# S5 output loads and conv-state stores moved from SyncE's queue to GpSimd's, with three buffers for the conv states

## Chip, cores and metric

The kernel runs on one core of one Trainium2 chip. The metric is the device time of one execution in microseconds (us); lower is better. A profile has times of the engines TensorE (PE, with PEld for its weight loads), VectorE (DVE), ScalarE (ACT), GpSimd (POOL) and SyncE (SP). SP computes nothing here; its queue issues transfers (DMAs), and so do parts of POOL's.

## What is computed

One layer of a hybrid decoder for 320 tokens (256 of a prompt, 8 samples of 8 tokens) of width 2048, in float32:

```python
def hybrid_layer(x, conv_buf, h_re, h_im, ...):
    xn = rmsnorm(x, norm_mix)
    proj = xn @ w_in
    c_val = proj[..., :D_CONV]
    c_gate = proj[..., D_CONV:2 * D_CONV]
    s_in = proj[..., 2 * D_CONV:]
    yc, new_buf = conformer_conv(c_val, c_gate, conv_buf, ...)
    ys, nh_re, nh_im = s5_mixer(s_in, h_re, h_im, ...)
    mix = jnp.concatenate([rmsnorm(yc, gnorm_conv), rmsnorm(ys, gnorm_ssm)], axis=-1) @ w_out
    h = x + mix.astype(x.dtype)
    hn = rmsnorm(h, norm_ffn)
    ff = (jax.nn.silu(hn @ w_ffn_gate) * (hn @ w_ffn_up)) @ w_ffn_down
    h = h + ff.astype(x.dtype)
    return h, new_buf, nh_re, nh_im
```

`conformer_conv` multiplies c_val by sigmoid(c_gate), runs a causal convolution of width 31 over each of 1024 channels, a LayerNorm over the channels and silu; `new_buf` holds the last 30 input rows of the convolution and is an output (the conv state). `s5_mixer` runs a complex diagonal state-space scan in 64 groups of 16 channels, and then `y = gelu(y)` and `y * sigmoid(y @ w_glu)`. A final norm follows the layer.

## The kernel before

Every matrix product is done with float32 split into a high and a low part. The weights come in "subs" of 1024 columns over 128 partitions: a transfer on SP's queue brings the raw weights (L124, four buffers), ACT copies the high part (`hi`, L141), DVE subtracts it for the low part (`lo`, L142), and 24 matmuls multiply high by high, high by low and low by high (L166 to L168) into `mm`. The subs follow each other for the input projection (`xhl` times w_in), the GLU (`gehl` times w_glu, 4 subs for each of two groups of columns), the output projection of the S5 half (`mid`) and of the convolution half (`half`, `half2`), and the FFN.

Beside the projection run the two mixers. The convolution works in eight chunks `c` of 128 channels (`conv_chunk`, L380 to L420). For each chunk ACT and PE build the window `u` (in a `ubuf`), and PE transposes the last 30 rows of each sequence (L392), which ACT copies to the tile `uo` (L394); two stores bring `uo` to the outputs (L395, L396). Chunks 3 and 5 then run their 31 taps on DVE (L438, into `convy`). The other six go to PE: four transfers copy shifted pieces of the window to `ub` (L402, one buffer), and 64 matmuls over the prompt (L410) and 64 over the samples (L414) add up the taps in `cx`, which ACT moves to `convy` (L419). `stn` (L377) is the load of the old conv state.

The S5 half works in eight blocks of 128 channels. Its end stores the block's result to DRAM (`yd`, L842). `gelu` (L864 to L883) then loads it back in another layout: at blocks 0 and 4 eight transfers of 16x32x40 each fill the tile `yl` with four blocks (L870), and for each block ACT and DVE compute the gelu (`gsq` L875 and L876, `gz` L878 and L879, `ge` L881) and split it into `gehl`, the high part on ACT (L882) and the low part on DVE (L883). The GLU's matmuls need `gehl`.

After the last chunk the convolution's LayerNorm runs (`ln_mean` to `ln_end`, on DVE and ACT). Each norm ends with small matmuls that sum over the channels (L324), a chain of small DVE steps for the reciprocal root (`rv` to `rg`, L303 to L328), small matmuls that spread it (L316) and a copy (L318, `Rc` for the convolution's last norm). The output projection's conv half needs `Rc` for its results (L1021).

Every engine and every queue does its instructions in the order in which a scheduler put them when the kernel was built. `when(slot)` gives an instruction its priority (a table of slots for the parts of the mixers, `P_CONV` and the like), and the scheduler places an instruction by that and by the time at which it expects the inputs. So a transfer that is moved to another queue also moves other instructions in the order of every engine. POOL's queue carries, beside small set-up work, transfers of the S5 half (`ud` L725, `us` L727, `KTd` L808, `tst` L812) and, late, four loads of `h` (L1001).

Of the kernel before, what the change touches and what calls it, by code (L numbers as in the profile page):

```python
# [8 lines left out]
F32 = mybir.dt.float32  # L9
# [52 lines left out]
def kernel(ctx: ExitStack, tc: tile.TileContext,  # L62
# [7 lines left out]
    V, A, G, T, SP = nc.vector, nc.scalar, nc.gpsimd, nc.tensor, nc.sync  # L70
# [3 lines left out]
    @contextmanager  # L74
    def when(slot):

        old = tc.cur_priority
        tc.cur_priority = int(BASE + slot * SLOT)
        yield
        tc.cur_priority = old  # L80
# [13 lines left out]
    def sx_tile(shape):  # L94
        return pss.tile(shape, F32, tag="sx", name="sx")

    def cx_tile(shape):
        return pss.tile(shape, F32, tag="cx", name="cx", bufs=1)
# [105 lines left out]
    def pv(i):  # L204
        return PV[:, i:i + 1]
# [4 lines left out]
    convp = cpool.enter_context(tc.tile_pool(name="convp", bufs=1))  # L210
# [169 lines left out]
    def conv_chunk(c):  # L380
        u = us_.pop(c)
        traced.add(("conv", c))
        stn = stn_.pop(c)
        win_ = u[:, 350:654].rearrange("p (b t) -> p b t", t=38)
        A.activation(win_[:, :, 30:38], u[:, 286:350].rearrange("p (b t) -> p b t", t=8), AF.Copy)
        pc = sx_tile([128, 368])
        ps = pc[:, 0:240].rearrange("p (h r) -> p h r", h=2)
        for h in range(2):
            T.transpose(ps[:, h, :], stn[:, h, :], ident[:120, :120])
        A.activation(win_[:, :, 0:30], ps.rearrange("p h (b t) -> p (h b) t", t=30), AF.Copy)  # L390
        ps = pc[:94, 240:368]
        T.transpose(ps, u[:, 256:350], ident)  # L392
        uo = convp.tile([94, 128], F32, name="uo", bufs=1)
        A.activation(uo, ps, AF.Copy)  # L394
        SP.dma_start(ncv_p[0, 0, :, c * 128:(c + 1) * 128], uo[0:30])  # L395
        SP.dma_start(ncv_s[0, :, 22:30, c * 128:(c + 1) * 128], uo[30:94])  # L396
        if c in V_CONV:
            return conv_taps_on_v(c, u, win_)

        ub = convp.tile([128, 4, UW - 24], F32, name="ub", tag="wide")  # L400
        for b in range(4):
            SP.dma_start(ub[:, b, :],  # L402
                         bass.AP(tensor=u.tensor, offset=u[32 * b:32 * b + 32].offset,
                                 ap=[[u.ap[0][0], 32], [8, 4], [1, UW - 24]]))
        cw = cw_.pop(c)
        with when(P_CONV[c]):
            acc = cx_tile([128, NTOK])
            for k in range(8):
                for b in (3, 2, 1, 0):
                    T.matmul(acc[32 * b:32 * b + 32, 0:256], cw[:, b, k, :], ub[:, b, k:k + 256],  # L410
                             start=(k == 0), stop=False, skip_group_check=True)
            for k in range(8):
                for b in range(4):
                    T.matmul(acc[32 * b:32 * b + 32, 256:320].rearrange("p (b t) -> p b t", t=8),  # L414
                             cw[:, b, k, :],
                             bass.AP(tensor=ub.tensor, offset=ub[:, b, 350 + k:351 + k].offset,
                                     ap=[list(ub.ap[0]), [38, 8], [1, 8]]),
                             start=False, stop=(k == 7), skip_group_check=True)
            A.activation(convy[:, c, :], acc, AF.Identity, bias=pv(CB + c))  # L419
        add_ysum(c)  # L420

    def add_ysum(c):
        if c == 0:
            V.tensor_copy(ysum, convy[:, 0, :])
        else:
            V.tensor_tensor(ysum, ysum, convy[:, c, :], op=OP.add)

    def conv_taps_on_v(c, u, win_):

        pairs = [(convy[:, c, 0:256], lambda k: u[:, k:k + 256]),  # L430
                 (convy[:, c, 256:320].rearrange("p (b t) -> p b t", t=8),
                  lambda k: win_[:, :, k:k + 8])]
        for dst, src in pairs:
            A.activation(dst, src(0), AF.Identity, bias=pv(CB + c), scale=convw[:, c, 0:1])  # L434
        for k in range(1, 31):
            with when(P_CONV[c] + V_CONV[c] * k):
                for dst, src in pairs:
                    V.scalar_tensor_tensor(dst, src(k), convw[:, c, k:k + 1], dst,  # L438
                                           op0=OP.mult, op1=OP.add)
        with when(P_CONV[c] + V_CONV[c] * 31):  # L440
            add_ysum(c)
# [422 lines left out]
    def gelu(b):  # L864
        gp = late["gp"]
        ge, gehl = late["ge"], late["gehl"]
        if b % 4 == 0:
            yls = late["yl"] = gp.tile([128, 32, 40], F32, name="yl", bufs=2)
            for g in range(8):
                SP.dma_start(yls[16 * g:16 * g + 16],  # L870
                             bass.AP(tensor=yd.tensor, offset=yd.offset + b * 128 * NTOK + 40 * g,
                                     ap=[[NTOK, 16], [16 * NTOK, 32], [1, 40]]))
        yl = late["yl"][:, 8 * (b % 4):8 * (b % 4) + 8]
        sq = gp.tile([128, 8, 40], F32, name="gsq", bufs=3)
        A.activation(sq, yl, AF.Square)  # L875
        A.activation(sq, sq, AF.Copy, bias=C0, scale=C0 * 0.044715)  # L876
        z = gp.tile([128, 8, 40], F32, name="gz", bufs=3)
        V.tensor_tensor(z, sq, yl, op=OP.mult)  # L878
        A.activation(z, z, AF.Sigmoid)  # L879
        gv = ge[:, b, :].rearrange("p (j t) -> p t j", t=8)[:, ::-1, :]  # L880
        V.tensor_tensor(gv, z, yl, op=OP.mult)  # L881
        A.activation(gehl[:, 0, b, :], ge[:, b, :], AF.Copy)  # L882
        V.tensor_tensor(gehl[:, 1, b, :], ge[:, b, :], gehl[:, 0, b, :].bitcast(F32), op=OP.subtract)  # L883
# [428 lines left out]
    def post(b):  # L1312
# [3 lines left out]

    job(n_proj, open_mid)
    parts_ = dict(v=pool_v, pre=pre, e=s5_e, w=pool_w, scan=s5_scan, post=post, gelu=gelu,
                  stn=conv_states, cw=conv_weights, conv=conv_chunk, sample=lambda b: s5_sample_states(),
                  incoming=lambda b: s5_incoming(),  # L1320
                  states=lambda b: s5_states(), open_g=lambda b: open_g(),
# [75 lines left out]
```

## Time and profile before

| | us |
|---|---|
| median of 3 runs | 1400.57 |
| lowest, highest run | 1400.56, 1404.74 |
| the profiled execution | 1397.38 |
| its span, first to last instruction | 1395.6 |
| mean granted TensorE clock in it | 0.993 |

The profile describes one execution. Its span lacks 1.78 us that lie around the first and the last instruction. An engine's busy time is the sum of its instructions; times in a timeline are counted from the span's start. In a timeline one row can stand for several instructions of the same form in a row (x8), and the brackets at its end give the idle time of the engine just before it and what ended that idle time. For a queue a row is the issue of a transfer, not its landing.

### The profile page before, as it was taken

What the parts mean: (1) busy time and instruction counts of PE and PEld (TensorE: products, weight loads), DVE (VectorE), ACT (ScalarE), POOL (GpSimd) and SP (SyncE); (2) the same over time, 40 slices, a digit from 0 to 9 for tenths busy, and PEclk for the clock granted to TensorE, in tenths of its full rate; (3) what the DMA queues carried; (4) which work ended last, traced back from release to release, by engine and by line L of the source; (5) the groups of instructions that cost most, each with busy time, mean ns of one, the idle gap of its engine ahead of it and who ended that gap; (6) DMA issues with size and microseconds to landing.
All of it is one profiled execution on the core that took longest, in us unless ns stands there. A gap on an engine that the chain in (4) does not pass through costs nothing.

```text
span 1395.6 us, 24894 instructions
## 1 busy us (share of the span) xinstructions
PE 1370.2 (98%) x10246; PEld 1341.8 (96%) x10246; DVE 827.2 (59%) x1523; ACT 557.2 (40%) x813; POOL 30.3 (2%) x61
## 2 busy tenths in 40 slices
PE   8999999899999999999999999999999999999996
PEld 7999988889999999999999999999999999999996
DVE  7988899887888543543454444343544444444465
ACT  7445444464545333333333333333332233333332
POOL 0121010000000000000000000000000000000000
PEclk9999999999999999999999999999999999999998
DMA  9974475767434444444444444444444444454442
GB/s 256 234 153 148 161 210 159 162 173 236 137 127 160 151 151 151 148 148 148 148 149 151 151 151 151 147 154 150 145 146 153 151 150 151 151 181 151 152 136 76
DMA packets 146586, 220.12 MB, mean 158 GB/s; under 512 B 32377, under 2 KB 57529, under 8 KB 146328
## 3 DMA queue, kind: packets, MB, share of 16 engines
q1 hardware_dynamic: 143336, 208.50, 48.6%
q0 software_dynamic: 3136, 10.03, 2.8%
q8 instruction: 80, 1.31, 0.4%
q14 instruction: 34, 0.28, 0.1%
HBM read 201.04 MB, written 10.41 MB: 152 GB/s over the span
## 4 chain that ended last, share of the span: by engine, by line
PE 79%; DMA 3%; DVE 2%; SPq 1%; ACT 1%; issue 0%; DVEq 0%; ACTq 0%
PE mm L166 25%; PE mm L167 25%; PE mm L168 25%; DMA ub<-ubuf 1%; PE cx L410 1%; DVE lo L142 1%; PE sx L831 0%; DMA yl<-yd 0%; SPq L402 0%; PE sx L836 0%; DVE ge L881 0%; DMA tst<-KTd 0%; DVE convy L438 0%; SPq L870 0%; PE cx L414 0%
## 5 line engine op out<-in xcount | busy, mean ns | idle before, releaser
L142 DVE TENSOR_TENSOR lo<-raw,hi 128x1024 fp32r<-128x1024 f32 x352 | 429.8, 1223 | 428.1 <-ACT hi L141 427.3
L141 ACT ACTIVATE hi<-raw 128x1024 fp32r<-128x1024 f32 x352 | 372.6, 1060 | 638.5 <-PE mm L167 579.3
L166 PE MATMUL mm<-hn,hi 128*128 128x320 f32 x1408 | 434.9, 309 | 0.0
L167 PE MATMUL mm<-hn,hi 128*128 128x320 f32 x1408 | 434.8, 309 | 0.0
L168 PE MATMUL mm<-hn,lo 128*128 128x320 f32 x1408 | 431.2, 309 | 0.0
L166 PEld LDWEIGHTS mm<-hn,hi 128*128 128x128 f32 x1408 | 264.3, 188 | 0.1
L167 PEld LDWEIGHTS mm<-hn,hi 128*128 128x128 f32 x1408 | 264.3, 188 | 0.0
L168 PEld LDWEIGHTS mm<-hn,lo 128*128 128x128 f32 x1408 | 263.3, 188 | 0.0
L166 PE MATMUL mm<-aout,hi 128*128 128x320 f32 (+1 forms) x704 | 216.7, 308 | 0.0
L167 PE MATMUL mm<-aout,hi 128*128 128x320 f32 (+1 forms) x704 | 216.3, 308 | 0.0
L168 PE MATMUL mm<-aout,lo 128*128 128x320 f32 (+1 forms) x704 | 213.9, 307 | 0.0
L167 PEld LDWEIGHTS mm<-aout,hi 128*128 128x128 f32 x704 | 132.2, 188 | 0.0
L166 PEld LDWEIGHTS mm<-aout,hi 128*128 128x128 f32 x704 | 132.2, 188 | 0.0
L168 PEld LDWEIGHTS mm<-aout,lo 128*128 128x128 f32 x704 | 131.5, 188 | 0.0
L167 PE MATMUL mm<-xhl,hi 128*128 128x320 f32 x384 | 119.7, 314 | 0.3 <-DVE xhl L274 0.3
L168 PE MATMUL mm<-xhl,lo 128*128 128x320 f32 x384 | 119.5, 314 | 0.0
L166 PE MATMUL mm<-xhl,hi 128*128 128x320 f32 x384 | 115.8, 315 | 0.5 <-DVE vt L964 0.3
L167 PEld LDWEIGHTS mm<-xhl,hi 128*128 128x128 f32 x384 | 72.1, 188 | 1.6 <-issue 0.6
L166 PEld LDWEIGHTS mm<-xhl,hi 128*128 128x128 f32 x384 | 70.6, 188 | 2.3 <-issue 0.8
L168 PEld LDWEIGHTS mm<-xhl,lo 128*128 128x128 f32 x384 | 72.0, 188 | 0.8 <-issue 0.2
L1100 DVE TENSOR_TENSOR h<-mm,h 128x320 f32<-128x320 f32 (+1 forms) x64 | 29.8, 483 | 39.9 <-PE mm L168 39.9
L438 DVE SCALAR_TENSOR_TENSOR convy<-ubuf,convw,convy 128x256 f32<-128x256 f32 (+1 forms) x120 | 41.5, 380 | 2.3 <-ACT convy L434 1.7
(333 smaller groups left out, 1361.9 us busy)
## 6 DMA issues: line engine op xcount, KB each, us to landing
raw<-in_w_ffn_gate_dram SPq DMA_DIRECT2D x88, 512.0 KB
raw<-in_w_ffn_up_dram SPq DMA_DIRECT2D x88, 512.0 KB
raw<-in_w_ffn_down_dram SPq DMA_DIRECT2D x88, 512.0 KB
raw<-in_w_in_dram SPq DMA_DIRECT2D x64, 256.0 KB
raw<-in_w_out_dram SPq DMA_DIRECT2D x32, 512.0 KB
raw<-in_w_in_dram SPq DMA_DIRECT2D x16, 512.0 KB
ub<-ubuf SPq DMA_DIRECT2D x24, 316.0 KB
tst<-KTd POOLq DMA_DIRECT2D x8, 512.0 KB, 5.2
```

The lines of the kernel that those rows point to most:

```text
L141: A.activation(hi, src, AF.Copy)
L142: V.tensor_tensor(lo, src, hi.bitcast(F32), op=OP.subtract)
L166: T.matmul(ps, wh, xh, start=(k == 0), stop=False)
L167: T.matmul(ps, wh, xl, start=False, stop=False)
L168: T.matmul(ps, wl, xh, start=False, stop=(k == g.nk - 1))
L410: T.matmul(acc[32 * b:32 * b + 32, 0:256], cw[:, b, k, :], ub[:, b, k:k + 256], start=(k == 0), stop=False, skip_group_check=True)
L438: V.scalar_tensor_tensor(dst, src(k), convw[:, c, k:k + 1], dst, op0=OP.mult, op1=OP.add)
L1100: V.tensor_tensor(hv, ps, hv, op=OP.add)
```

## The change

The two stores of a conv state and the loads of the S5 results are issued from POOL's queue (`G`) and not from SP's, and the tile `uo` has three buffers and not one:

```diff
     def conv_chunk(c):
...
-        uo = convp.tile([94, 128], F32, name="uo", bufs=1)
+        uo = convp.tile([94, 128], F32, name="uo", bufs=3)
         A.activation(uo, ps, AF.Copy)
-        SP.dma_start(ncv_p[0, 0, :, c * 128:(c + 1) * 128], uo[0:30])
-        SP.dma_start(ncv_s[0, :, 22:30, c * 128:(c + 1) * 128], uo[30:94])
+        G.dma_start(ncv_p[0, 0, :, c * 128:(c + 1) * 128], uo[0:30])
+        G.dma_start(ncv_s[0, :, 22:30, c * 128:(c + 1) * 128], uo[30:94])
...
     def gelu(b):
...
             for g in range(8):
-                SP.dma_start(yls[16 * g:16 * g + 16],
+                G.dma_start(yls[16 * g:16 * g + 16],
                              bass.AP(tensor=yd.tensor, offset=yd.offset + b * 128 * NTOK + 40 * g,
                                      ap=[[NTOK, 16], [16 * NTOK, 32], [1, 40]]))
```

That is 16 loads and 16 stores. SP's queue has 158 entries before and 130 with the change, POOL's 35 and 55; a stretch of equal transfers is one entry. In the rows below the numbers behind a name tell tiles of the same name apart.

**SP's queue, and POOL's, at the end of the projection.** `raw_3850` is the first of the GLU's weights, `ub_3333` the pieces of chunk 4's window, `yl_3250` and `yl_3445` the two tiles of S5 results, `uo_3329` the conv state of chunk 4. SP before:

```order
L124 DMA raw_3850<-in_w_glu_dram 128x2x512
L402 DMA ub_3333<-ubuf0_111 128x1x632
L870 DMA yl_3250<-yd_123 16x32x40 x4
L124 DMA raw_3884<-in_w_glu_dram 128x2x512
L870 DMA yl_3250<-yd_123 16x32x40 x4
L395 DMA out_2_dram<-uo_3329 30x128
L396 DMA out_5_dram<-uo_3329 8x8x128
L124 DMA raw_3914<-in_w_glu_dram 128x2x512
L402 DMA ub_3333<-ubuf0_111 128x1x632 x3
L870 DMA yl_3445<-yd_123 16x32x40 x2
```

SP with the change, from the same load of weights:

```order
L124 DMA raw_3850<-in_w_glu_dram 128x2x512
L402 DMA ub_3333<-ubuf0_111 128x1x632 x4
L124 DMA raw_3884<-in_w_glu_dram 128x2x512
L377 DMA stn_3766<-in_state_conv_dram 120x2x128
L124 DMA raw_3914<-in_w_glu_dram 128x2x512
L124 DMA raw_3944<-in_w_glu_dram 128x2x512
L124 DMA raw_4091<-in_w_glu_dram 128x2x512
```

The four pieces of `ub_3333` stood apart, with eight loads of `yl`, two stores and two loads of weights between the first and the other three; now the four stand together, and the weights follow. POOL before, at its end:

```order
L812 DMA tst_2581<-KTd_124 128x8x128
L812 DMA tst_2648<-KTd_124 128x8x128
L812 DMA tst_2762<-KTd_124 128x8x128
L812 DMA tst_2977<-KTd_124 128x8x128
L1001 DMA h_4247<-xTd_90 128x1280 x4
```

POOL with the change, from the last of the same loads of `tst`:

```order
L812 DMA tst_2977<-KTd_124 128x8x128
L395 DMA out_2_dram<-uo_2797 30x128
L396 DMA out_5_dram<-uo_2797 8x8x128
L395 DMA out_2_dram<-uo_2910 30x128
L396 DMA out_5_dram<-uo_2910 8x8x128
L870 DMA yl_3250<-yd_123 16x32x40 x8
L870 DMA yl_3445<-yd_123 16x32x40 x6
L395 DMA out_2_dram<-uo_3329 30x128
L396 DMA out_5_dram<-uo_3329 8x8x128
L870 DMA yl_3445<-yd_123 16x32x40 x2
L395 DMA out_2_dram<-uo_3469 30x128
L396 DMA out_5_dram<-uo_3469 8x8x128
```

The sixteen loads of `yl` stand in one row, with one pair of stores before the last two; six more rows of stores and the four loads of `h` follow.

**PE, the matmuls of chunk 4 at the end of the projection.** The projection's last matmuls are those on `xhl`. Before:

```order
L168 MATMUL mm_3291<-xhl_89,lo_3724 128x320
L166 MATMUL mm_3298<-xhl_89,hi_3723 128x320
L410 MATMUL cx_3338<-ub_3333,cw_3321 32x256 x32
L414 MATMUL cx_3338<-ub_3333,cw_3321 32x64 x32
L167 MATMUL mm_3298<-xhl_89,hi_3723 128x320
L168 MATMUL mm_3298<-xhl_89,lo_3724 128x320
L166 MATMUL mm_3298<-xhl_89,hi_3723 128x320
L167 MATMUL mm_3298<-xhl_89,hi_3723 128x320
L168 MATMUL mm_3298<-xhl_89,lo_3724 128x320
```

With the change:

```order
L167 MATMUL mm_3291<-xhl_89,hi_3661 128x320
L168 MATMUL mm_3291<-xhl_89,lo_3662 128x320
L166 MATMUL mm_3298<-xhl_89,hi_3661 128x320
L167 MATMUL mm_3298<-xhl_89,hi_3661 128x320
L168 MATMUL mm_3298<-xhl_89,lo_3662 128x320
L410 MATMUL cx_3338<-ub_3333,cw_3321 32x256 x32
L414 MATMUL cx_3338<-ub_3333,cw_3321 32x64 x32
L166 MATMUL mm_3298<-xhl_89,hi_3661 128x320
L167 MATMUL mm_3298<-xhl_89,hi_3661 128x320
```

The 128 matmuls of chunk 4 stand 46 places earlier in PE's order; 57 of the projection's matmuls now follow them, where 11 did, before the GLU begins. Chunk 7's, which stood after the first matmuls of the output projection, also stand 46 places earlier and so inside the GLU.

**PE, the last norm of the convolution (L324 to L316).** Before, the sums over the channels stand among these rows; from them to the L316 of the same norm 34 matmuls follow:

```order
L168 MATMUL mm_4972<-half2_4349,lo_5063 128x320
L166 MATMUL mm_4972<-half2_4349,hi_5062 128x320
L167 MATMUL mm_4972<-half2_4349,hi_5062 128x320
L324 MATMUL sx_4455<-ones1k_87,lnt_4350 128x1 x2
L324 MATMUL sx_4455<-ones1k_87,lnt_4350 64x1
L168 MATMUL mm_4972<-half2_4349,lo_5063 128x320
L168 MATMUL mm_4979<-half2_4349,lo_5063 128x320
L166 MATMUL mm_4979<-half2_4349,hi_5062 128x320
```

With the change:

```order
L168 MATMUL mm_5128<-half2_4349,lo_5159 128x320
L324 MATMUL sx_4455<-ones1k_87,lnt_4350 128x1 x2
L324 MATMUL sx_4455<-ones1k_87,lnt_4350 64x1
L166 MATMUL mm_5128<-half2_4349,hi_5188 128x320
L167 MATMUL mm_5128<-half2_4349,hi_5188 128x320
L168 MATMUL mm_5128<-half2_4349,lo_5189 128x320
L166 MATMUL mm_5128<-half2_4349,hi_5188 128x320
L167 MATMUL mm_5128<-half2_4349,hi_5188 128x320
L168 MATMUL mm_5128<-half2_4349,lo_5189 128x320
L316 MATMUL sx_4478<-ident_78,rg_4463 128x128 x2
L316 MATMUL sx_4478<-ident_78,rg_4463 128x64
```

The sums stand 28 places later; between them and L316 lie 6 matmuls and not 34.

On DVE 20 rows (taps L438, one `cw` L369 and one sum L426) stand ahead of the first `gz` (L878) with the change that stood behind it before.

## Rows read from the trace of the kernel before

**Rows 1.** The page: busy time by engine; cost of a weight's lo step.
```profile
PE 1370.2 (98%) x10246; PEld 1341.8 (96%) x10246; DVE 827.2 (59%) x1523; ACT 557.2 (40%) x813; POOL 30.3 (2%) x61
...
L142 DVE TENSOR_TENSOR lo<-raw,hi 128x1024 fp32r<-128x1024 f32 x352 | 429.8, 1223 | 428.1 <-ACT hi L141 427.3
```

**Rows 2.** Waits of PE, 196 to 345 us: us in total, times, longest.
```profile
PE cx L410 <- DMA ub<-ubuf: 8.4, 5, 3.9
```

**Rows 3.** Windows: width, PE, PEld, DVE, ACT, POOL busy, PEclk, DMA share, GB/s.
```profile
265.00:270.00 5.00, 5.00 (x36) 5.00 (x35) 1.28 (x5) 2.42 (x8) 0.00 (x0) 1.00 0.72 191
270.00:275.00 5.00, 1.26 (x9) 1.00 (x7) 5.00 (x12) 4.53 (x10) 0.00 (x0) 0.92 0.89 180
275.00:280.00 5.00, 4.79 (x48) 2.66 (x52) 5.00 (x13) 0.98 (x3) 0.00 (x0) 0.50 1.29 191
```

**Rows 4.** Timeline of PE, 266 to 285 us: start, us, work, idle before.
```profile
270.95 0.31 PE L166 MATMUL mm<-xhl,hi 128*128 128x320 f32 x1
275.21 6.51 PE L410 MATMUL cx<-ub,cw 128*32 128x256 f32 x64 [3.95 <-DMA ub<-ubuf]
...
284.31 0.31 PE L166 MATMUL mm<-gehl,hi 128*128 128x320 f32 x1
```

**Rows 5.** Timeline of PE, 302 to 327 us.
```profile
304.30 3.67 PE L410 MATMUL cx<-ub,cw 128*32 128x256 f32 x64 [1.42 <-DMA ub<-ubuf]
...
323.06 3.68 PE L410 MATMUL cx<-ub,cw 128*32 128x256 f32 x64 [0.93 <-DMA ub<-ubuf]
```

**Rows 6.** Timeline of SP's queue, 196 to 342 us, same columns.
```profile
255.09 0.65 SPq L402 DMA_DIRECT2D ub<-ubuf  x1
256.31 3.19 SPq L870 DMA_DIRECT2D yl<-yd  x4
...
260.07 2.54 SPq L870 DMA_DIRECT2D yl<-yd  x4
262.71 2.27 SPq L395 DMA_DIRECT2D out_dram<-uo  x1
...
266.27 3.30 SPq L402 DMA_DIRECT2D ub<-ubuf  x3
...
273.39 3.55 SPq L870 DMA_DIRECT2D yl<-yd  x5
...
277.53 0.38 SPq L870 DMA_DIRECT2D yl<-yd  x1
```

**Rows 7.** Timeline of ACT, 234 to 300 us.
```profile
236.25 0.27 ACT L394 ACTIVATE uo<-sx 94x128 f32<-94x128 f32 x1 [1.84 <-DMA out_dram<-uo]
...
267.58 1.19 ACT L875 ACTIVATE gsq<-yl 128x320 f32<-128x320 f32 x3 [4.42 <-DMA out_dram<-uo]
...
281.42 1.19 ACT L875 ACTIVATE gsq<-yl 128x320 f32<-128x320 f32 x3 [4.90 <-DMA yl<-yd]
```

**Rows 8.** Timeline of POOL, 50 to 110 us.
```profile
52.35 5.16 POOL L725 DMA_DIRECT2D ud<-s_in  x8 [17.42 <-DVE pw L468]
69.64 2.18 POOL L727 DMA_DIRECT2D us<-ud  x4 [12.12 <-DMA ud<-s_in]
...
90.35 5.00 POOL L725 DMA_DIRECT2D ud<-s_in  x8 [3.79 <-DVE s_in L718]
...
105.71 2.14 POOL L727 DMA_DIRECT2D us<-ud  x4 [9.22 <-DMA ud<-s_in]
```

**Rows 9.** Timeline of DVE, 255 to 300 us.
```profile
269.33 0.49 DVE L878 TENSOR_TENSOR gz<-gsq,yl 128x320 f32<-128x320 f32 x1 [3.72 <-ACT gsq L876]
...
277.46 0.48 DVE L883 TENSOR_TENSOR gehl<-ge,gehl 128x320 fp32r<-128x320 f32 x1
```

**Rows 10.** Timeline of DVE, 395 to 410 us.
```profile
398.79 0.15 DVE L327 TENSOR_SCALAR rv<-sx 128x2 f32<-128x2 f32 x1
...
404.88 0.49 DVE L318 COPY Rc<-sx 128x320 f32<-128x320 f32 x1 [1.49 <-PE sx L316]
```

**Rows 11.** Timeline of PE, 398 to 408 us.
```profile
405.95 0.42 PE L166 MATMUL mm<-half,hi 128*128 128x320 f32 x1 [1.10 <-DVE t L1021]
```

## Prediction, made before the changed kernel was run

> **What bounds the kernel now.** I read the page first: PE is busy 1370.2 of 1395.6 us [rows 1], so time can come only out of what PE waits for, out of slower matmuls, or out of the work itself. The change touches no matmul. It moves transfers that PE meets in one stretch, from about 196 us, where the convolution and the S5 mixer run beside the projection, to about 405 us, where the last norm ends. So I went on to PE's waits in the first part of it: one item is large, the shifted window pieces `ub` that the tap matmuls L410 need, 8.4 us over five waits, 3.9 us the longest [rows 2]. PE's timeline shows three of these: 3.95 us before chunk 4 at 275.21, 1.42 before chunk 6 at 304.30, 0.93 before chunk 7 at 323.06 [rows 4, 5]. The windows show what the longest one does beside standing still: PE is busy 1.26 of 5 us, and in the next 5 us the granted clock is 0.50 where it was 1.00 (1.2 GHz after 2.4), so that the same 64 matmuls take 6.51 us and not the 3.67 of chunk 6 [rows 3 to 5].
>
> Why is `ub` late for chunk 4? SP's queue tells: it issues the first of four pieces at 255.09, and the other three only at 266.27, after eight loads of `yl` (3.19 and 2.54 us of issuing), the wait for the conv state at 262.71 (2.27 us) and two loads of weights [rows 6]. The pieces are ready to be issued; they stand behind others.
>
> **The change part by part.** *The four pieces of chunk 4.* With the change SP issues them together behind `raw_3850`. From 255.09, at 0.65 us each, the last is issued by 257.7. Before, the three pieces were issued by 269.57 and PE went on at 275.21, 5.6 us later [rows 4, 6]; so they land at about 263.3. If the landing takes as long as from the first of the three issues, 8.9 us, it is 264.6. PE comes to chunk 4 earlier too, by 46 matmuls. One takes 0.14 us (36 in 5.00 us, [rows 3]), 46 take 6.4, so PE is there at about 264.9 where it was there at 271.3 (275.21 − 3.95). The wait goes: 3.95 us. With no idle stretch ahead of it the chunk runs at the full clock: 6.51 − 3.67 = 2.84 us. Both ends of the price of this part: 0, if the pieces land as late as before, and 6.8.
>
> *Chunks 6 and 7.* No `yl` load and no store stands ahead of their pieces. I take their 1.42 and 0.93 us as gone; they could also stay.
>
> *Three buffers for `uo`.* ACT waited 1.84 us at 236.25 for an earlier store out of the only buffer [rows 7]. That wait cannot stay with three. A transpose of PE stands behind it, so some of it reached PE; I take 0.4, between 0 and 1.84. At 267.58 the timeline names the same store for ACT's 4.42 us, but the next thing ACT does there is the gelu on `yl`, and that has its own data to wait for: eight loads from 256.31. I take nothing for it.
>
> These come to 3.95 + 2.84 + 1.42 + 0.93 + 0.4 = 9.5 us. They are kept only if what PE reaches earlier is ready.
>
> *The GLU.* PE would start it at 284.31 − 6.8 = 277.5 [rows 4]. It needs `gehl`, whose source `yl` is now loaded by POOL, all sixteen transfers in a row. POOL never loaded `yl` before, so I bound it. Below: SP's own eight, from 256.31 to ACT's first step at 267.58, 11.3 us, and the last load of the second group landed 3.9 us after its issue (277.53 to 281.42) [rows 6, 7]. Above: POOL's loads of `ud`, eight of nearly the same shape, from 52.35 to 69.64 and from 90.35 to 105.71, so 17.3 and 15.4 us until the next step could go [rows 8]. I take 13.5 for the first eight, nearer to SP's, since tile, source and place are the same and only the queue differs: ACT starts on it at 269.8 and not 267.6. The 3.9 us of landing is paid once in a row of sixteen, so a group beyond it costs 7.4 us (SP), 11.5 or 13.4 (POOL), 9.6 by my choice. The sixteenth then lands at 256.3 + 3.9 + 2 × 9.6 = 279.4, with ends at 275.0 and 287.0. Before, ACT started on the second group at 281.42: that half is not later.
>
> So the first `gz` comes 1.75 us after ACT's start as before, at 271.6, and the first low part of `gehl` 8.6 us behind it (269.33 to 277.94, [rows 9]), at 280.2. PE, there at 277.5, waits 2.7 us where it did not. Behind that, 20 DVE rows that lay between the gelu's steps lie ahead of them, and the weights' `lo` steps shift among them: I add two such steps, 2 × 1.22 us [rows 1], for the parts that PE now meets earlier; the ends are 0 and the whole 6.8 − 2.7 = 4.1 that PE is still ahead. Cost: 2.7 + 2.4 = 5.1 us.
>
> *The last norm.* Before, 34 matmuls (4.8 us) lay between L324 and L316 and covered the DVE chain from 398.79 to `Rc` at 404.88 all but 1.10 us [rows 10, 11]. Now 6 do (0.8 us): 4.0 us of cover are gone. But the sums stand 28 matmuls later, so their input may long be there and the 4.0 us come back by PE having done more. Only if the norm's chain on DVE and ACT is as late as before is PE's lead lost here. I take 1.5 of a possible 0 to 4.4.
>
> *POOL's other work.* The loads of `h` stand behind all the stores now; they were issued far ahead of their use. The stores end in outputs that nothing reads. Nothing for both; should POOL be late with `h`, it would show as a wait of the output projection.
>
> *The sum.* −9.5 + 5.1 + 1.5 = −2.9 us. The profiled execution took 1397.38 us, 3.2 below the median of the three runs; against itself that is 1394.5, against the median 1397.7. I forecast **1397.7 us**. About 0.3%, 4.2 us, is what a measurement of this kernel can tell from no change, so this counts as none.
>
> A rule speaks against this change. The 16 DMA engines have shares of 0.72, 0.89 and 1.29 in the three windows from 265 to 280 us [rows 3], so they are nearly full or over-full there (overlapping packets count twice). The Trainium skill, "DMA: Bandwidth & Descriptors", section "Issuing engines are not separate DMA queues", says that transfers from all engines end up on the same 16 DMA engines, and that issuing from several saves only the issuing time. By that rule the 11 us between the first and the second issue of `ub` are still saved, but the pieces would not land sooner than their share of those engines allows; the third rival below works that out.
>
> **The rivals.** *The gain is kept.* If the gelu gets its `yl` at SP's pace (267.6) and DVE, with the taps out of its way, turns it into `gehl` in less than 8.6 us, the GLU's wait is 0 to 2 us, and the norm gives nothing back: −6 to −9.5, **1391 to 1394.5**. For it: DVE stood idle 3.72 us before the first `gz` [rows 9], so the moved rows may cost nothing. Against: everything after has to be early as well. 0.22.
>
> *`yl` comes late: slower.* POOL's loads go at the pace of `ud`, and every group of eight pays its 15.4 to 17.3 us whole, since the second can't be issued freely while the first is under way: the sixteenth lands between 287.1 and 290.9. Each microsecond behind 281.4 stops PE in the GLU for one, as nothing but the GLU's own second half is left there. 5.7 to 9.5 us late, less the 2.9: +2.8 to +6.6, about **1405**. It decides from a landing at 281.4 + 2.9 + 4.2 = 288.5 us. For it: both batches of `ud` took that long. Against: they ran in another stretch with other traffic. 0.16. The rows show a POOL issue of 0.65 us for `ud` (5.16 for eight) [rows 8], and DVE busy for 5.00 of 5 us when `yl` is under way [rows 3]. The Trainium skill, "SBUF — State Buffer", section "SBUF: two separate sides", warns that a transfer issued from GpSimd waits for its descriptors while DVE runs an operation in a mode that holds the port the two share. By that rule this rival would be likelier than I put it; but what fills DVE there are two-input forms at their usual length, and no row yet shows such a stop.
>
> *The DMA engines are the limit.* The pieces land as late as before, with eight loads of `yl` beside them: PE waits about 4 us for chunk 4, only 46 matmuls earlier, the half clock comes with it, and 0.4 to 2 us are gained elsewhere: **1399 to 1400.5**. 0.12.
>
> *The norm takes it all.* PE's lead of 4.4 us is given back in front of L316: **1400.5**. 0.10.
>
> **How the numbers follow.** My forecast, with some 2.5 us to either side, has 0.40; of that 0.13 lies beyond −4.2. Faster by over 0.3%: 0.13 + 0.22 = 0.35. Slower by over 0.3%: most of the second rival and a little of the unforeseen, 0.15. Within: 0.50. The range reaches from the far part of the first rival, 1391.0, to the middle of the second, 1404.5; about 0.06 lies below and 0.10 above.
>
> **What would show it.** Right: the four `ub` issues of chunk 4 together near 255 us and no wait before its L410, all 64 in some 3.7 us, the clock at 1.00 through 265 to 285; a new wait of 2 to 3 us of the GLU's first matmul for `gehl`; ACT's first gelu step near 270, the second group's before 281.5; some PE wait at L316 near 400 us. Wrong: `yl` landing behind 285, PE's wait for `ub` still there, or the GLU starting below 278 without a wait and the lead kept to 405 us.

## The result, and the profile after

The changed kernel takes 1413.58 us (median of 9 runs, 1407.86 to 1416.85), the kernel before 1400.92 in the same comparison (9 runs). One of those nine took 4733.93 us and is left out of the ratio, which is 1.0076 with a 95% interval of 1.0059 to 1.0094. The medians lie 12.7 us apart; by the ratio the change is some 10.6 us slower. A second comparison gave 1.0066 (1.0041 to 1.0092). The forecast of 1397.7 us and its range up to 1404.5 were both wrong.

The profiled execution of the change has a span of 1411.8 us, 16.2 more than before. PE's line on the page answers to [rows 1]:

```profile
PE 1380.8 (98%) x10246; PEld 1348.2 (96%) x10246; DVE 828.0 (59%) x1523; ACT 557.0 (39%) x813; POOL 49.4 (3%) x93
```

PE does the same 10246 matmuls and is busy 10.6 us longer, at a mean granted clock of 0.987 where it was 0.993: most of this trace's 16.2 us is matmuls at half the clock, and the rest are waits. PE's timeline tells where. I took four points of the program that both kernels pass: the first tap matmul of chunk 1 (A) and of chunk 2 (B), the end of the last `mid` matmul (D) and of the last `half` matmul (E), with the GLU's first matmul (C) between B and D:

| us | A to B | B to C | C to D | D to E |
|---|---|---|---|---|
| before | 27.95 | 48.48 | 102.09 | 59.71 |
| change | 32.05 | 49.57 | 106.22 | 66.45 |
| change, second trace | 28.44 | 49.58 | 105.93 | 65.25 |

A to B is left out of what follows. In the first trace of the change the clock falls there to 0.52 after a wait of 1.31 us, in the second it doesn't after 1.34 us, and in the kernel before it didn't after 1.35 us; PE's order is the same in all three up to there. From B to E the change loses 12.0 and 10.5 us, about what the ratios say: 1.1 before the GLU, 4.1 (3.8) in the GLU and the S5 half of the output projection, 6.7 (5.5) in the convolution's half.

**At chunk 4.** The windows (columns as in [rows 3]) show the same two stretches as before, and two new ones:

```profile
210.00:215.00 5.00, 5.00 (x28) 4.75 (x31) 5.00 (x16) 1.97 (x5) 0.00 (x0) 0.52 0.42 131
...
265.00:270.00 5.00, 3.62 (x25) 3.33 (x24) 4.88 (x13) 1.26 (x2) 2.71 (x5) 1.00 1.05 199
270.00:275.00 5.00, 0.82 (x8) 0.45 (x12) 4.24 (x15) 0.00 (x0) 2.79 (x5) 0.66 1.07 190
275.00:280.00 5.00, 5.00 (x78) 2.87 (x74) 0.00 (x0) 1.19 (x3) 2.07 (x4) 0.65 1.10 154
410.00:415.00 5.00, 3.93 (x26) 3.38 (x25) 2.15 (x10) 1.06 (x1) 0.00 (x0) 1.00 0.31 107
415.00:420.00 5.00, 2.23 (x7) 1.85 (x8) 2.70 (x12) 0.00 (x0) 0.00 (x0) 0.50 0.30 105
420.00:425.00 5.00, 5.00 (x20) 5.00 (x20) 4.77 (x13) 2.85 (x7) 0.00 (x0) 0.50 0.00 0
```

PE again has an empty stretch near 270 us and the half clock with it; the pieces of chunk 4 are still late. PE's timeline, with the rows that wait in the GLU:

```profile
274.18 5.75 PE L410 MATMUL cx<-ub,cw 128*32 128x256 f32 x64 [5.56 <-DMA ub<-ubuf]
...
291.01 0.41 PE L167 MATMUL mm<-gehl,hi 128*128 128x320 f32 x1 [0.72 <-DVE gehl L883]
...
297.19 0.42 PE L167 MATMUL mm<-gehl,hi 128*128 128x320 f32 x1 [0.38 <-DVE gehl L883]
...
299.63 0.41 PE L166 MATMUL mm<-gehl,hi 128*128 128x320 f32 x1 [1.00 <-ACT hi L141]
...
302.00 0.42 PE L168 MATMUL mm<-gehl,lo 128*128 128x320 f32 x1 [1.16 <-DVE lo L142]
```

The wait before chunk 4 is 5.56 us where it was 3.95 [rows 4], its matmuls take 5.75 us where they took 6.51, and four waits in the GLU (3.3 us in all) are new. One trace says little about a difference of 1 us here: the second trace of the change has 5.14, and norm_late (below), with the queues and the order of before up to there, 5.01. The waits before chunks 6 and 7 [rows 5] are gone in this trace; the second has 1.33 us before chunk 6. SP's queue issued the four pieces together, as the order says, and POOL's queue the loads of `yl` beside them. First SP, then POOL:

```profile
259.19 5.71 SPq L402 DMA_DIRECT2D ub<-ubuf  x4
265.00 0.74 SPq L124 DMA_DIRECT2D raw<-in_w_glu_dram  x1
...
266.64 28.29 SPq L124 DMA_DIRECT2D raw<-in_w_glu_dram  x5
...
315.42 4.95 SPq L402 DMA_DIRECT2D ub<-ubuf  x4
```

```profile
261.24 4.97 POOL L870 DMA_DIRECT2D yl<-yd  x8 [23.22 <-ACT uo L394]
...
278.31 0.63 POOL L870 DMA_DIRECT2D yl<-yd  x1 [0.90 <-DMA yl<-yd]
```

The issues begin at 259.19 and end at 264.90; PE goes on at 274.18, 9.3 us later, where it was 5.6 before. Four pieces in a row take SP nearly as long where no `yl` load is under way, 4.95 us at 315.42. The sixteen `yl` loads are out between 261.24 and 278.94.

**At the gelu.** ACT and DVE stand in this order in the change:

```profile
275.14 1.19 ACT L875 ACTIVATE gsq<-yl 128x320 f32<-128x320 f32 x3 [7.68 <-DMA yl<-yd]
280.96 0.53 ACT L419 ACTIVATE convy<-cx,PV 128x320 f32<-128x320 f32 x1 [4.63 <-PE cx L414]
281.39 1.18 ACT L876 ACTIVATE gsq<-gsq 128x320 f32<-128x320 f32 x3
```

```profile
268.44 5.80 DVE L438 SCALAR_TENSOR_TENSOR convy<-ubuf,convw,convy 128x256 f32<-128x256 f32 x19
280.96 1.23 DVE L369 TENSOR_TENSOR cw<-tapw,blkmask 128x1024 f32<-128x1024 f32 x1 [6.72 <-PE cx L414]
...
283.29 1.29 DVE L878 TENSOR_TENSOR gz<-gsq,yl 128x320 f32<-128x320 f32 x3
```

`yl` is in at 275.14, 13.9 us after its first issue. But the gelu's second step (L876) stands on ACT behind L419, the copy of chunk 4's result, and the first `gz` on DVE behind L369, which needs the buffer that chunk 4's matmuls read. So ACT waits 4.63 us and DVE 6.72 us, at the same time, for PE's chunk 4, which itself waits for the pieces. The first `gz` comes 8.15 us behind ACT's start on `yl`, where it came 1.75 us behind it before [rows 7, 9]: the gelu is late by some 6.4 us. Before, L419 stood behind the second group's first steps.

**At the last norm.** PE's timeline from the sums (L324) to the spreading (L316):

```profile
411.88 0.71 PE L324 MATMUL sx<-ones1k,lnt 128*128 128x1 f32 x6
...
414.03 0.42 PE L168 MATMUL mm<-half,lo 128*128 128x320 f32 x1 [0.95 <-DVE lo L142]
...
416.66 1.81 PE L316 MATMUL sx<-ident,rg 128*128 128x128 f32 x6 [1.78 <-DVE rg L308]
419.58 0.64 PE L166 MATMUL mm<-half,hi 128*128 128x320 f32 x1 [1.11 <-DVE t L1021]
```

Before, PE met 1.10 us of waiting there [rows 11]; now it is 0.95 + 1.78 + 1.11, with DVE's chain between, and in the windows above the clock is 0.50 from 415 to 425 us. The norm's own steps are later too. Its last addition on DVE (L946) and the chain's first step stand at:

```profile
408.89 1.08 DVE L946 TENSOR_TENSOR lnt<-lnt 128x320 f32<-128x320 f32 x2
412.62 0.16 DVE L327 TENSOR_SCALAR rv<-sx 128x2 f32<-128x2 f32 x1 [2.65 <-PE sx L324]
```

The sums' input is ready at 409.97, 14.1 us behind D, and PE comes to the sums 1.9 us after that; before, it was ready 8.0 us behind D.

### The profile page after: what moved, and what is told of

It is laid out like the page before. It is cut to its first block, busy times and chain, and to the rows that moved or that the text cites. A ratio compares the mean times of both kernels' runs of the same rounds, so it can differ in the third digit from the quotient of the medians.

```text
span 1411.8 us, 24898 instructions
## 1 busy us (share of the span) xinstructions
PE 1380.8 (98%) x10246; PEld 1348.2 (96%) x10246; DVE 828.0 (59%) x1523; ACT 557.0 (39%) x813; POOL 49.4 (3%) x93
## 3 DMA queue, kind: packets, MB, share of 16 engines
q8 instruction: 80, 1.31, 0.4%
## 4 chain that ended last, share of the span: by engine, by line
PE 78%; DVE 3%; DMA 2%; issue 1%; ACT 1%; SPq 0%; DVEq 0%; ACTq 0%; POOLq 0%
PE mm L168 25%; PE mm L166 25%; PE mm L167 25%; PE cx L410 1%; DMA ub<-ubuf 1%; DVE lo L142 1%; DVE convy L438 0%; DMA tst<-KTd 0%; SPq L402 0%; PE sx L316 0%; PE sx L1148 0%; PE cx L414 0%; DVE convy L937 0%; DVE ge L881 0%; ACT yt L1212 0%
## 5 line engine op out<-in xcount | busy, mean ns | idle before, releaser
L438 DVE SCALAR_TENSOR_TENSOR convy<-ubuf,convw,convy 128x256 f32<-128x256 f32 (+1 forms) x120 | 40.1, 378 | 2.1 <-ACT convy L434 1.5
```

## The experiments

Names and numbers of instructions are the same in both kernels, so the order of an engine can be written down from one build and held in another. The first edit adds an edge from each instruction to the one ahead of it in such a list; it orders the issue alone and makes nothing wait for data:

```diff
     with when(len(subs) + 1):
         tail_end()
+    pin_order(tc)
...
+        for d in json.loads(zlib.decompress(base64.b85decode(packed))):
+            n += d
+            i = by.get(f"I-{n}")
...
+            if prev is not None:
+                tc.add_manual_dep(i, prev.name, mybir.DependencyInfo(
+                    mybir.DependencyClass.NoSync, mybir.DependencyReason.DATA),
+                    reason="order")
+            prev = i
```

**pin_order: the change's queues, the order of before on PE, DVE and ACT.**

> The changed queues and the three buffers, with PE, ACT and DVE held to the order of before (same instructions in the same row on each); SP's and POOL's queues stand here as in the change from the first GLU weights to the second last one. Theory A (the new order on PE, ACT and DVE costs the time): 1396 to 1403 us, the four pieces of chunk 4 issued near 255 to 260 us, chunk 4 back behind the 46 matmuls with a wait under 4 us, no wait at L316 near 400 us. Theory B (the loads on POOL's queue cost it, in whatever order): 1408 to 1415 us, waits of the GLU's matmuls for gehl of 4 us or more.

**rev_order: the queues of before, the change's order on PE, DVE and ACT.** Theory A, that the order costs the time, was my theory from the profile; theory B is the rival of the prediction that forecast a slower kernel.

> The queues and the one buffer of before, with PE, ACT and DVE held to the order of the change. Theory A (order): 1408 to 1416 us, with the wait at L316 and a half clock behind it near 415 us as in the change, and chunk 4's wait for its pieces longer than the 3.95 us of before, since PE is there 46 matmuls earlier. Theory B (loads on POOL): 1398 to 1404 us.

**loads_only and stores_only: half of the change each**, with the order that the scheduler makes of it:

```diff
-                SP.dma_start(yls[16 * g:16 * g + 16],
+                G.dma_start(yls[16 * g:16 * g + 16],
```

```diff
-        uo = convp.tile([94, 128], F32, name="uo", bufs=1)
+        uo = convp.tile([94, 128], F32, name="uo", bufs=3)
...
-        SP.dma_start(ncv_p[0, 0, :, c * 128:(c + 1) * 128], uo[0:30])
-        SP.dma_start(ncv_s[0, :, 22:30, c * 128:(c + 1) * 128], uo[30:94])
+        G.dma_start(ncv_p[0, 0, :, c * 128:(c + 1) * 128], uo[0:30])
+        G.dma_start(ncv_s[0, :, 22:30, c * 128:(c + 1) * 128], uo[30:94])
```

> Only the loads of yl on POOL's queue; conv states as before, one buffer, and the order that results. Theory A: what its order makes of it; the row of PE differs little from the change's (68 lines against 478 from before), so 1408 to 1415 us. Theory B: the same 1408 to 1415 us. Were the stores the cause, 1398 to 1404 us.

> Only the conv states' stores on POOL's queue, with three buffers; yl loaded on SP. Theory B (loads on POOL): 1396 to 1402 us. Theory A: PE's row differs from before's in 414 lines, so it may be slower too, 1403 to 1412 us, if the last norm's sums stand late in it.

Measured, as ratios to before with intervals: pin_order 1.0018 (0.9995 to 1.0040), rev_order 1.0141 (1.0109 to 1.0173), loads_only 1.0106 (1.0069 to 1.0143), stores_only 1.0101 (1.0065 to 1.0136). With the queues of the change and the order of before, nearly the whole loss is gone; with the queues of before and the order of the change it is larger than the change's. Theory A stands, theory B falls. In microseconds all four lie above what I had expected for theory A (1404.60, 1422.81, 1417.91 and 1417.66, with the kernel before at 1403.46), so their sizes were missed. In rev_order PE waits 9.89 us for chunk 4's pieces: it comes there early, and SP still sends them late. stores_only, which leaves every `yl` load on SP, is as slow: it also gets a new order, and all four traces with a new order have D to E at 65.5 to 66.5 us. pin_order has 59.73. Chunk 4's matmuls are not early in stores_only; before chunk 6 PE waits 3.49 us there, where it was 1.42 before [rows 5]. That its order and not its stores cost the time was not run by itself; ub_first (below), with the same stores on POOL and the order of before, loses nothing.

pin_order also answers the question about chunk 4. PE's timeline in it:

```profile
273.59 3.69 PE L410 MATMUL cx<-ub,cw 128*32 128x256 f32 x64
...
280.61 0.38 PE L166 MATMUL mm<-gehl,hi 128*128 128x320 f32 x1 [0.57 <-issue]
284.39 0.63 PE L167 MATMUL mm<-gehl,hi 128*128 128x320 f32 x1 [3.40 <-DVE gehl L883]
...
295.86 0.31 PE L392 MATMUL sx<-ident,ubuf 128*94 128x128 f32 x1 [1.84 <-DVE ubuf L972]
```

With PE at its old place in the order, the four pieces are in time: no wait, 3.69 us at the full clock, and the GLU's first matmul is 43.45 us behind B, 5.0 less than before. The gain of chunk 4 is real. Then PE waits 3.40 us for `gehl` and 1.84 us for a window, runs 3.4 us at half the clock, and at D all of it is given back: B to D is 151.79 us, 1.2 more than before.

**The parts of the order.** Five runs put one part of the order back, or in. The edit is the same, with another list.

**norm_late: before, with the change's order from behind the S5 norm on.**

> The kernel before with its queues and one buffer, its order up to the S5 norm, and the order of the change from there on: nothing differs but where the convolution's norm stands among the output projection's matmuls (6 matmuls between L324 and L316). If that place costs what the traces say: 6 to 7 us, ratio 1.004 to 1.005, a wait at L316 of some 1.8 us and half the clock for some 10 us behind it. If not: 1.000 and no stretch at 0.50 near 410 us.

Measured: 1.0037 (1.0017 to 1.0057). The order behind the S5 norm costs some 5 us by itself, a little less than expected; D to E is 66.49 us. More than the place of the sums differs in it: the matmuls of both halves, ACT's and DVE's steps of the norm and the steps behind it stand in another order too, and the sums' input is ready 14.1 us behind D as in the change. PE's timeline and a window:

```profile
408.12 0.71 PE L324 MATMUL sx<-ones1k,lnt 128*128 128x1 f32 x6
...
412.90 1.81 PE L316 MATMUL sx<-ident,rg 128*128 128x128 f32 x6 [1.78 <-DVE rg L308]
415.82 0.64 PE L166 MATMUL mm<-half,hi 128*128 128x320 f32 x1 [1.11 <-DVE t L1021]
```

```profile
415.00:420.00 5.00, 4.18 (x16) 4.18 (x17) 4.71 (x12) 2.35 (x6) 0.00 (x0) 0.50 0.00 0
```

The same 1.78 us at L316, and the half clock with it.

**change_again: the change once more**, beside conv_norm_back (below).

> The change once more, on the same chip as the run above: ratio 1.006 to 1.010. Its trace shows a second time the wait at L316 and the half clock behind it; whether the half clock from 210 to 219 us, which the first trace has and the one of before has not though PE's row is the same there, comes again or not tells if it belongs to the change.

Measured: the 1.0066 and the second trace given above. The half clock in A to B did not come again, the one at L316 did.

**norm_back: the change, with the order of before from the S5 norm's sums on.**

> The change, with its queues and its order on PE, DVE and ACT up to the sums of the S5 norm (chunk 4 46 matmuls early, the GLU's new order), and the order of before from there on, so that 34 matmuls lie again between L324 and L316 of the convolution's last norm. If the late sums of that norm are one of two causes, worth the 6 to 7 us by which that stretch is longer in all four traces with the new order: 6 to 7 us below the change, a ratio to before of 1.003 to 1.006. If the convolution and the GLU alone are the cause: as the change, 1.0076 or more. If the norm is all of it: 1.000.

**conv_norm_back: the same, but with the S5 norm left where the change has it.**

> The change, with its queues and its order on PE, DVE and ACT through the S5 norm, and the order of before from there on; unlike the run norm_back, the S5 norm's own sums stay where the change has them, so PE doesn't meet them early. Two causes: 5 to 7 us below the change run beside it, ratio to before 1.003 to 1.005, no wait at L316 and no half clock near 415 us. If the convolution and the GLU are all of it: as the change.

Measured: 1.0087 (1.0060 to 1.0113) and 1.0079 (1.0062 to 1.0096); my expectation missed both times. D to E is 61.25 and 59.70 us, as it should be, but B to D grew by 6.0 and 6.1 us over the change's. PE's timelines, first norm_back, then conv_norm_back:

```profile
340.32 1.31 PE L324 MATMUL sx<-ones1k,ssum 128*128 128x1 f32 x6 [3.55 <-DVE ssum L899]
```

```profile
359.21 0.46 PE L166 MATMUL mm<-mid,hi 128*128 128x320 f32 x1 [4.26 <-DVE t L1008]
```

In norm_back PE comes to the S5 norm's sums before `ssum` is there, 3.55 us; in conv_norm_back it waits 4.26 us for results (`t`, L1008) that DVE evacuates behind the convolution's norm. With the GLU late, the old place of the norm is too early for its neighbours. Neither run gets the 5 us back alone.

**chunk4_back: the change, with PE's matmuls of chunk 4 back behind the 46.**

> The change with one thing undone: the 128 matmuls of chunk 4 stand on PE behind the 46 matmuls again, as before; DVE and ACT keep the order of the change. If the wait for the pieces and the half clock behind it are what the early place costs: no wait before chunk 4, its matmuls in 3.7 us, 4 to 7 us below the change (ratio to before 1.002 to 1.005). If ACT's and DVE's rows of chunk 4 (L419, L369, L426), which stand ahead of the gelu's steps, are what holds the GLU: PE is early at the GLU and waits there for gehl by as much, and the time stays at the change's, ratio 1.006 to 1.010.

Measured: 1.0085 (1.0060 to 1.0110), no gain. PE's and ACT's timelines:

```profile
281.36 3.69 PE L410 MATMUL cx<-ub,cw 128*32 128x256 f32 x64
...
292.30 0.60 PE L166 MATMUL mm<-gehl,hi 128*128 128x320 f32 x1 [3.46 <-ACT gehl L882]
...
295.92 0.63 PE L167 MATMUL mm<-gehl,hi 128*128 128x320 f32 x1 [0.90 <-DVE gehl L883]
```

```profile
281.19 1.19 ACT L875 ACTIVATE gsq<-yl 128x320 f32<-128x320 f32 x3 [7.65 <-DMA yl<-yd]
286.09 0.53 ACT L419 ACTIVATE convy<-cx,PV 128x320 f32<-128x320 f32 x1 [3.71 <-PE cx L414]
286.52 1.18 ACT L876 ACTIVATE gsq<-gsq 128x320 f32<-128x320 f32 x3
```

Chunk 4 no longer waits, and B to C, with the wait of 3.46 us for `gehl` at its end, is 3.4 us shorter than in the change. C to D is 4.0 us longer, most of it by the clock: it is 0.50 from 295 to 300 us, behind that wait. On ACT L876 still stands behind L419 and waits 3.71 us for PE. ACT's and DVE's order was not put back alone; that the engines would then wait for each other in a circle, with chunk 4 early on PE, is argued and not shown.

**early_back: the change, with all three engines in the order of before up to the S5 norm.**

> The change's queues and three buffers, with PE, DVE and ACT in the order of before up to the S5 norm (chunk 4 behind the 46 matmuls, and its rows on ACT and DVE behind the gelu's steps), and in the order of the change from there on. chunk4_back put back PE's part of the early order and gained nothing; if ACT's and DVE's rows are the rest of it, this run loses only what norm_late lost: ratio 1.003 to 1.006, ACT's step L876 directly behind L875 without L419 between. If the early part isn't held by those rows: 1.0076 or more.

Measured: 1.0048 (1.0024 to 1.0071), an interval that overlaps both of the change's, so what is won back is read from the traces. B to D is 152.30 us, 1.7 more than before and 3.5 less than the change. ACT's steps follow each other:

```profile
274.72 1.19 ACT L875 ACTIVATE gsq<-yl 128x320 f32<-128x320 f32 x3 [8.06 <-DMA yl<-yd]
...
275.97 1.17 ACT L876 ACTIVATE gsq<-gsq 128x320 f32<-128x320 f32 x3
```

What is left is the last norm, D to E 65.65 us. So, from B to E: 7.0 us with the order behind the S5 norm alone (norm_late), 7.7 with that order and the change's queues (early_back), 12.0 with all of it.

**The row of SP's queue.** Five runs hold PE, DVE and ACT to the order of before, and write SP's row by hand. All but the last have the stores of conv states on POOL with three buffers. The rows behind `raw_3850`: ub_first has the four pieces, eight `yl`, `raw_3884`, eight `yl`; ub_first_both the same, and chunk 2's pieces ahead of the `yd` store that stood among them, where they stay in the three that follow; yl_ub_yl has eight `yl`, the four pieces, four `yl`, `raw_3884`, four `yl`; yl_ub_raw_yl has `raw_3884` ahead of all eight of the second group. sp_only has the same, with nothing moved to POOL and one buffer; its row against that of before:

```diff
 L124 DMA raw_3850<-in_w_glu_dram 128x2x512
-L402 DMA ub_3333<-ubuf0_111 128x1x632
-L870 DMA yl_3250<-yd_123 16x32x40 x4
-L124 DMA raw_3884<-in_w_glu_dram 128x2x512
-L870 DMA yl_3250<-yd_123 16x32x40 x4
+L870 DMA yl_3250<-yd_123 16x32x40 x8
+L402 DMA ub_3333<-ubuf0_111 128x1x632 x4
 L395 DMA out_2_dram<-uo_3329 30x128
 L396 DMA out_5_dram<-uo_3329 8x8x128
-L124 DMA raw_3914<-in_w_glu_dram 128x2x512
-L402 DMA ub_3333<-ubuf0_111 128x1x632 x3
-L870 DMA yl_3445<-yd_123 16x32x40 x2
+L124 DMA raw_3884<-in_w_glu_dram 128x2x512
+L870 DMA yl_3445<-yd_123 16x32x40 x8
...
```

> PE, DVE and ACT in the order of before; the conv states' stores on POOL's queue with three buffers; yl on SP, but behind the four pieces of chunk 4. If the pieces were late only for standing behind others on SP: no wait before chunk 4, its matmuls in 3.7 us, the GLU's first matmul some 4 to 7 us before 284.3, then a wait of it for gehl of 2 to 4 us, in all 1 to 4 us faster than before (ratio 0.997 to 0.999). If the DMA engines are the limit: yl is later by what the pieces gain, no change or up to 3 us slower.

> As the last, and the four pieces of chunk 2 ahead of one store of y that stood among them. Chunk 2's wait (0.8 to 1.6 us) and the half clock behind it (some 3 us) go if that store was what made them late: 2 to 4 us faster than the last; else the same.

> PE, DVE and ACT in the order of before; conv states' stores on POOL with three buffers, chunk 2's pieces together; on SP the first eight loads of yl ahead of chunk 4's four pieces, and the second eight behind them. If what bounds the stretch is which transfer the DMA engines serve first: yl's first group in by 267 us, the pieces by 271, no wait before chunk 4, the GLU's first matmul near 278 us with a wait for gehl under 2 us, 3 to 6 us faster than before (ratio 0.996 to 0.998). If the pieces land after 274: a wait again, no gain.

> As yl_ub_yl, with the second load of GLU weights ahead of all eight of the second yl loads; ACT waited 4.26 us for that load there, with the gelu's steps behind it. If that wait reached PE: PE's waits in the GLU (0.42, 0.64 and 2.06 us) shrink, 1 to 3 us below yl_ub_yl, ratio to before 0.995 to 0.997. If not: 0.997 to 0.999.

> Nothing on POOL's queue and one buffer for the conv states, as before; only SP's row is written anew: the first eight yl loads, chunk 4's four pieces, its conv state, the second GLU weights, the second eight yl loads, and chunk 2's pieces together. If the place of the transfers in the row is what counts and not the queue that issues them: as yl_ub_raw_yl within 0.2%, ratio to before 0.995 to 0.999. If the stores in SP's row hold up what stands behind them: 1.000 or more.

| run | ratio to before (95%) | B to D | D to E |
|---|---|---|---|
| ub_first | 1.0007 (0.9992 to 1.0023) | 151.93 | 61.24 |
| ub_first_both | 0.9996 (0.9981 to 1.0010) | 149.16 | 59.70 |
| yl_ub_yl | 0.9977 (0.9959 to 0.9995) | 146.78 | 61.24 |
| yl_ub_raw_yl | 0.9973 (0.9955 to 0.9990) | 145.01 | 59.70 |
| sp_only | 0.9970 (0.9955 to 0.9986) | 148.05 | 59.71 |

Pieces first gives nothing that these runs can tell from no change: `yl` is later by what they gain. I had expected 2 to 4 us of chunk 2's pieces; by the ratios ub_first_both is 1.5 below ub_first, inside the intervals. The first `yl` group ahead of the pieces and the second behind them, with chunk 2's pieces together, gives about 0.25% (the first without the second was not run), and sp_only shows that this needs neither POOL's queue nor the buffers. Its SP row and PE:

```profile
260.37 0.41 SPq L124 DMA_DIRECT2D raw<-in_w_glu_dram  x1
262.13 4.04 SPq L870 DMA_DIRECT2D yl<-yd  x8
266.27 4.86 SPq L402 DMA_DIRECT2D ub<-ubuf  x4
271.24 0.68 SPq L395 DMA_DIRECT2D out_dram<-uo  x1
...
273.42 0.46 SPq L124 DMA_DIRECT2D raw<-in_w_glu_dram  x1
273.93 7.01 SPq L870 DMA_DIRECT2D yl<-yd  x8
```

```profile
276.98 3.70 PE L410 MATMUL cx<-ub,cw 128*32 128x256 f32 x64
...
283.28 0.31 PE L166 MATMUL mm<-gehl,hi 128*128 128x320 f32 x1
285.21 0.41 PE L167 MATMUL mm<-gehl,hi 128*128 128x320 f32 x1 [1.62 <-DVE gehl L883]
...
296.71 0.32 PE L392 MATMUL sx<-ident,ubuf 128*94 128x128 f32 x1 [1.42 <-DVE ubuf L972]
```

The pieces are all issued by 271.13, PE meets no wait before chunk 4, and the GLU waits 1.62 us. In this trace, and in those of yl_ub_yl and yl_ub_raw_yl, the clock fell in A to B, and PE comes to chunk 4 some 5 us later by it; whether it meets no wait otherwise is not shown. sp_only is faster than both kernels: 1399.81 us, against 1403.86 for the kernel before in that comparison, 0.30% (0.14% to 0.45%). The wait of 4.26 us on ACT that yl_ub_raw_yl was to remove fell to 2.12 us, and that was worth no more than the interval.

## Why the prediction was wrong

*What bounds the kernel*: right. The empty stretch before chunk 4 was there to be won, and pin_order won 5.0 us of it where I had put 6.8.

*The four pieces of chunk 4*: this step failed first. I put it at a gain of 6.8 us; from B to the GLU the change lost 1.1. I let the pieces land 5.6 us behind their last issue, at 263.3. The last issue ended at 264.90, 5.7 us after the first where I had 2.6, and PE went on 9.3 us behind it. For the issuing I took four times the 0.65 us of a single piece, though my own rows had 3.30 us for three in a row [rows 6]; sp_only needs 4.86 us for four with nothing of this on POOL. The landing came from a stretch in which SP issued one transfer after the other, and the change puts eight `yl` loads beside the pieces. What I had as a rival ("the DMA engines are the limit") holds for the landing. As PE also comes 46 matmuls earlier, the wait stayed, at 5.56 us. But chunk4_back shows that this place by itself costs nothing in the end while ACT and DVE keep their rows: what PE does not wait for there it waits for at `gehl`.

*Chunks 6 and 7, and the buffers*: 2.35 us of waits were to go; the first trace bears that out, the second has 1.33 us left. ACT's wait for the conv state's store is gone in both, but sp_only, with one buffer, has two of over 3 us and is as fast as yl_ub_raw_yl: the 0.4 us that I took for it show nowhere.

*The GLU*: the landing of `yl` was sized well (13.5 us forecast for the first eight, 13.9 measured; the sixteenth landed at about 287, 26.1 us behind the first issue, where I had 23.1 and an upper end of 30.7). What I missed is in the rows that I had counted: I took the "20 DVE rows" ahead of the gelu as work and priced them at two steps of 1.22 us. Among them are L369 and L426, and L419 on ACT, which need chunk 4's matmuls. They don't cost their length; they tie the gelu to the transfer that the change was to speed up. early_back, which puts back the whole early order of the three engines, wins 3.5 us between B and D.

*The last norm*: I took 1.5 us of a possible 0 to 4.4, and it costs 5 to 7 (D to E grew by 6.7 and 5.5). Of that 2.6 us are waits, at the place where the cover that I had counted went (34 matmuls, now 6); norm_late, with the order behind the S5 norm alone, has the same. The upper end that I gave was for a norm as late as before on DVE and ACT; the sums' input came 6.1 us later behind D. Which of the moved rows does it was not run apart. My bound missed the half clock at the stop, some 2.9 to 4.1 us (what PE's matmuls from D to E take longer), though I had priced just that at chunk 4. And I took the early and the late part as two terms of a sum. norm_back and conv_norm_back show that they aren't: with the GLU late, undoing the norm's place moves the wait to its neighbours.

*The rivals*: the second had the sign, with 2.8 to 6.6 us where 10.6 were measured, and for the wrong reason. POOL's queue with the old order costs 0.18%, with an interval that takes in no change at all. The Trainium skill, "DMA: Bandwidth & Descriptors", section "Issuing engines are not separate DMA queues", says that issuing from several engines saves no more than the issuing time. For the stores, sp_only beside yl_ub_raw_yl (0.9970 and 0.9973) agrees. The Trainium skill, "SBUF — State Buffer", section "SBUF: two separate sides", warns that POOL's issues stop while DVE runs an operation in a mode that holds the port the two share. Such a stop was not seen: eight issues took 4.97 us, 0.63 each, while DVE ran its two-input forms. None of the runs was made to test another form.

What stays open: how much of the 3.5 us of the early part is ACT's rows and how much DVE's, as the two were not put back apart. Whether a stop lets the clock fall is not settled by these runs either: A to B is the same row of PE in all kernels, and the stretch was at half the clock in some executions and not in others.

## What to carry to other kernels

Where a scheduler orders the engines, moving a few transfers to another queue is a change to the order of every engine. Compare that order first, and look in it for instructions that now stand ahead of a chain and wait for the transfer concerned, and for norms that have lost the matmuls that covered them. Before giving transfers a second queue, write the row of the first one by what is needed when; here that row alone gave more than the second queue, and the same stores and loads could stay where they were. And a stop of PE is priced with the half clock that can follow it.

## What the runs showed of the hardware that I had not expected

Four pieces of 316 KB in a row took SP 5.71 us to issue, 0.63 and 0.59 us for the first two and 2.17 for each of the others. Eight POOL loads of 80 KB ran beside them, but those are not the cause of most of it: in the same trace four pieces took 4.95 us at 315.42, in sp_only 4.86, and before the last of three took 1.96 of their 3.30 us [rows 6]. What rose beside the loads is the landing behind the last issue: 9.0 to 10.4 us in the five traces in which PE waits for the four pieces with POOL's `yl` loads beside them, at a DMA share of 0.92 to 1.10 in the change, against 4.6 to 5.6 in before, rev_order and norm_late, at most 5.9 in sp_only and at most 5.6 in yl_ub_yl, and 7.0 in stores_only, where SP's own `yl` loads follow.

After the stops near 415 us (about 3.8 us of idle PE from 410 to 420) PE ran at 0.50 of its clock up to 425; the mean granted clock from 395 to 430 us is 0.85 to 0.92 in all eight traces with the late norm, and 0.95 or 1.00 in the nine others. After the stop at A the clock fell in some executions and not in others: it fell after 1.31 us in the change, and not after 1.34 in its second trace; it fell after 1.75 in loads_only, and not after 1.77 in early_back.
